# The gate and up stages of a macaron encoder layer: the sums of h taken kind by kind on VectorE, and three direct column blocks in the first stage instead of four

## The chip, the cores and the metric

One core of a Trainium2 chip runs the whole layer in one launch. The metric is the device time of that launch in microseconds, the median of several executions. Engines are named as the profile names them: PE is TensorE, DVE is VectorE, ACT is ScalarE, POOL is GpSimd, and SP is the engine that issues most of the DMAs. L619 and the like are lines of the kernel before.

## The reference, cut to what matters

One layer, batch 1, 1024 tokens, model width 1024, feed-forward width 2816. Three sandwiches follow each other, and the first and the last are feed-forward stages:

```python
def swiglu(h, w_gu, w_down):
    g, u = jnp.split(h @ w_gu, 2, axis=-1)
    return (jax.nn.silu(g) * u) @ w_down

def sandwich(x, fn, g_pre, g_post, shift, scale, gate, res_w):
    h = modulate(rmsnorm(x, g_pre), shift, scale)
    y = rmsnorm(fn(h), g_post)
    return x + res_w * gate[:, None, :] * y
...
x = sandwich(x, ffn1, ...)   # res_w 0.5
x = sandwich(x, mix, ...)    # attention and a recurrent branch
x = sandwich(x, ffn2, ...)   # res_w 0.5
```

The change lies in `h @ w_gu` of both feed-forward stages: `h` is 1024 x 1024, `w_gu` is 1024 x 5632. All is float32.

## The kernel before, in words

Every float32 operand is cut into a high part (an fp32r copy, ScalarE) and a low part (the value less its copy, mostly VectorE), and a product is three matmuls: high by high, low by high, high by low. `hh[k]` and `hl[k]` are the two parts of the k-th 128 rows of `h` transposed, 128 x 1024 (`h1` the first 512 tokens, `h2` the second). The columns of `w_gu` are taken in 22 column blocks `fb` of 128, gate and up together, of which `load` fetches 512 KB for each.

The first blocks are *direct*: `part(fb, sh, k)` (L582) does the six matmuls of one k on one half `sh` of the tokens, so a block has 2 x 8 x 6 = 96 matmuls of 128x128 by 128x512. `finish` (L599) applies Silu on ScalarE, the product with the up half on VectorE, and stores the result. `DIRECT` (L44) says how many: four in the first stage, three in the last. In the first stage blocks 0 to 2 belong to `startup` (L1679), since `h` is only being made; block 3 is done by `up_phase` (L794). In the last stage blocks 0 and 1 are done by `head` (L775), which runs beside the stage ahead of it.

All other blocks are done in Strassen's manner (`block`, L733; the Winograd form). Split in two over rows and tokens, seven products do the work of eight: `product(fb, i, ...)` (L725) has 4 x 3 = 12 matmuls, a block 7 x 12 = 84. The products stand in the order 1, 2, 6, 5, 7, 3, 4 (`ORDER`, L504). They need
- combinations of the weights, made by `mix(fb, i)` (L700): GpSimd adds and subtracts (four 128x512 instructions a block), ScalarE copies the high part, VectorE subtracts for the low part (seven times, L720). `mix(fb + 1, i)` is called in block `fb` after its product i;
- combinations of `h`, made once a stage by `sums()` (L616). With w, x the two token halves of the upper row block `kk` and y, z those of the lower one, kind 5 is x - w, kind 6 is z - (x - w), kind 4 is y - kind 6, and a fourth, z - x, goes by `differences(kk)` (L679) into `hh[kk]`, `hl[kk]`, second half, in place of x. Each of the first three is cut into a tile `hs` (`high` on ScalarE, `low` on VectorE). Product 5 needs kind 5, product 6 kind 6, product 4 kind 4, product 7 the differences.

Three PSUM banks carry a block. Products 1, 6, 7 and 4 go into one of them, `psX`, one after the other, and between them it is read out: ScalarE copies it to `u` after product 1 (L745) and to `v` after product 6 (L752), and VectorE adds it to `pp` after product 7 (L759, recorded as L739, the line of the helper). Product 6, 7 and 4 wait for these three. Product 3 goes into `psZ` after product 5 has been copied out to `pp` by ScalarE (L756).

In the first stage `h` in 32 bits is not kept. `sums()` has GpSimd add `hh` and `hl` back together (`whole`, L619: eight adds of 128x1024, at L623), and VectorE then does all four combinations of one kk before the next. The steps are spread by `sum_step()` over block 1's and 2's second halves (in `startup`, at the end) and block 3's first half; `first_needs` (L812) does what is left, the first seven mixes and the differences in block 3's second half. In the last stage the second half of `h` is kept in 32 bits from the time when it is made (`whole_h`, filled by `evac_h`, L353), and VectorE adds the first half together itself (L639).

The order of each engine's instructions is that in which this code issues them (`manual_schedule`); an engine takes its instructions strictly in that order. Another user of GpSimd in the stage is `all_sums` (L894), which makes combinations of the down-projection's weights and of finished blocks for the stage that follows; `block` calls `next(jobs)` after each product, and each call is at most one GpSimd instruction of 128x512 (L928).

The lines that matter in the profile: L349 cuts `h`, L143/L144 cut the weights of a direct block (ScalarE, and GpSimd for block 3 in the first stage), L486 to L488 are the direct matmuls, L729 to L731 those of the products, L521 is `finish` on VectorE.

Of the kernel before, what the change touches and what calls it, by code (L numbers as in the profile page):

```python
# [10 lines left out]
F32 = mybir.dt.float32  # L11
# [15 lines left out]
KB = D // P  # L27
# [16 lines left out]
DIRECT = {0: 4, 2: 3}  # L44
# [6 lines left out]
def kernel(  # L51
# [301 lines left out]
    def evac_h(sub, sh, k, pt, hh, hl, on_act, with_lo=True, eng=None):  # L353
# [152 lines left out]
    def ffn(sub, w_gu, w_down, hh, hl, xin, xout):  # L506
# [109 lines left out]
        def sums():  # L616
            recon = {}

            def whole(kk):  # L619
                if kk < 4:  # L620
                    recon[kk] = top, bot = t4("top"), t4("bot")
                    for dst, k in ((top, kk), (bot, kk + 4)):
                        nc.gpsimd.tensor_tensor(dst, hh[k].bitcast(F32), hl[k].bitcast(F32), op=ALU.add)  # L623

# [8 lines left out]
            if sub == 2:  # L633
                for kk in range(4):
                    top, bot = whole_h.pop(kk), whole_h.pop(kk + 4)
                    w_, x_, y_, z_ = top[:, h1], top[:, h2], bot[:, h1], bot[:, h2]
                    s1, s2 = tv("hsum"), tv("hsum")
                    for dst, k in ((w_, kk), (y_, kk + 4)):
                        nc.vector.tensor_tensor(dst, hh[k][:, h1].bitcast(F32), hl[k][:, h1].bitcast(F32), op=ALU.add)  # L639
# [5 lines left out]
                    nc.vector.tensor_tensor(z_, z_, x_, op=ALU.subtract)  # L645
                    dif[kk] = z_
                    nc.vector.tensor_tensor(y_, y_, s2, op=ALU.subtract)
                    high(4, kk, y_)
                    yield
                    low(5, kk, s1)  # L650
                    low(6, kk, s2)
                    low(4, kk, y_)
                    yield
                return

            whole(0)
            yield
            for kk in range(4):
                top, bot = recon.pop(kk)
                w_, x_, y_, z_ = top[:, h1], top[:, h2], bot[:, h1], bot[:, h2]  # L660
                s1, s2 = tv("hsum"), tv("hsum")
                nc.vector.tensor_tensor(s1, x_, w_, op=ALU.subtract)
                high(5, kk, s1)
                whole(kk + 1)
                nc.vector.tensor_tensor(s2, z_, s1, op=ALU.subtract)
                high(6, kk, s2)
                yield
                low(5, kk, s1)
                nc.vector.tensor_tensor(y_, y_, s2, op=ALU.subtract)
                high(4, kk, y_)  # L670
                yield
                low(6, kk, s2)
                nc.vector.tensor_tensor(z_, z_, x_, op=ALU.subtract)
                yield
                low(4, kk, y_)
                dif[kk] = z_
                yield

        def differences(kk):  # L679
            nc.scalar.copy(hh[kk][:, h2], dif[kk])  # L680
            nc.vector.tensor_tensor(hl[kk][:, h2], dif[kk], hh[kk][:, h2].bitcast(F32), op=ALU.subtract)
# [93 lines left out]
        def head():  # L775
# [11 lines left out]
            cut(2, 0)  # L787
            cut(2, 1)
            for k in range(KB):
                part(1, 1, k)  # L790
                sum_step()
            finish(1, 1, tu)
# [1134 lines left out]
```

## Time and profile before

| | |
|---|---|
| three runs | 2188.63, 2191.61, 2191.58 us; median 2191.58 |
| the profiled execution | 2188.63 us, of which 2186.8 from its first to its last instruction |
| PE busy | 2144.6 us, 98% |
| DVE busy | 1306.5 us, 60% |
| ACT busy | 1014.0 us, 46% |
| POOL busy | 699.9 us, 32% |
| mean granted TensorE clock | 0.997 |
| first stage, first direct matmul to first Strassen product | 22.28 to 129.21 us |
| one Strassen block without waits | 84 matmuls, 19.1 us |

How to read it: in a timeline, a row has the start and the length in us, the engine, the line, what is written and read, and in brackets how long the engine stood idle before it and what ended that. A matmul's own length (0.39 us) overlaps the next one's; the pace is the distance between starts. In the list of waits a row has who waited for what, the total in us, how often, and the longest.

### The profile page before, as it was taken

How to read it: one execution, taken by the hardware profiler on the slowest of the kernel's cores; microseconds unless marked ns; L12 is line 12 of the kernel's file. 1: busy time of each engine (PE TensorE's matmuls, PEld its weight loads, DVE VectorE, ACT ScalarE, POOL GpSimd, SP SyncE). 2: the span in 40 equal slices, each digit the busy share in tenths (PEclk: the TensorE clock that was granted, in tenths of full speed). 3: DMA queues.
4: the chain of work that ended last, by engine and by line, in shares of the span. 5: the costliest groups of instructions: out<-in, count | busy, mean ns of one | idle time of the engine just before them, and what ended most of it. 6: DMA issues, size and time to landing. Idle time of an engine off the chain costs nothing. (4 is left out here: it accounts for less than half of the span.)

```text
span 2186.8 us, 26725 instructions
## 1 busy us (share of the span) xinstructions
PE 2144.6 (98%) x9973; PEld 1780.1 (81%) x9973; DVE 1306.5 (60%) x1676; ACT 1014.0 (46%) x1570; POOL 699.9 (32%) x514
## 2 busy tenths in 40 slices
PE   7999999999999999999999999999999999999998
PEld 5878788888878888888898988888888888888877
DVE  6676676557367677655236666555686564544466
ACT  4343333334447788611147776436443333334443
POOL 1558895422104111000121120002168884522102
PEclk9999999999999999999999999999999999999999
DMA  9347674459575111276411011464357663347365
GB/s 327 88 164 256 225 260 154 154 192 335 185 249 195 51 51 43 60 241 218 138 49 61 26 56 55 135 207 164 111 192 260 236 219 118 109 151 271 132 232 183
DMA packets 259322, 358.36 MB, mean 164 GB/s; under 512 B 16592, under 2 KB 166264, under 8 KB 259192
## 3 DMA queue, kind: packets, MB, share of 16 engines
q1 hardware_dynamic: 246272, 310.43, 43.0%
q10 hardware_dynamic: 12920, 46.23, 5.4%
q8 instruction: 78, 1.28, 0.2%
q14 instruction: 52, 0.43, 0.1%
HBM read 265.37 MB, written 94.37 MB: 165 GB/s over the span
## 5 line engine op out<-in xcount | busy, mean ns | idle before, releaser
L143 ACT CAST dh<-rawd 128x1024 fp32r<-128x1024 f32 x154 | 161.4, 1054 | 203.3 <-PE pv L990 60.4
L720 DVE TENSOR_TENSOR wm<-raw,wm 128x512 fp32r<-128x512 f32 x152 | 161.0, 1064 | 153.6 <-ACT wm L719 148.3
L144 DVE TENSOR_TENSOR dh<-rawd,dh 128x1024 fp32r<-128x1024 f32 x130 | 163.1, 1259 | 148.1 <-ACT dh L143 139.2
L486 PE MATMUL pj<-hh,wh 128*128 128x512 f32 x574 | 226.4, 395 | 0.0
L487 PE MATMUL pj<-hl,wh 128*128 128x512 f32 x574 | 224.8, 392 | 0.7 <-DVE hl L349 0.6
L488 PE MATMUL pj<-hh,wl 128*128 128x512 f32 x574 | 224.9, 392 | 0.3 <-DVE wl L144 0.3
L990 PE MATMUL px<-dh,dh 128*128 128x512 f32 x608 | 187.5, 390 | 0.5 <-DVE dh L144 0.5
L338 POOL TENSOR_SCALAR rstd<-rstd 128x1 f32<-128x1 f32 x47 | 29.9, 637 | 429.0 <-ACT junk L337 427.6
L990 PE MATMUL pv<-dh,dh 128*128 128x512 f32 x528 | 163.1, 390 | 2.5 <-DVE dh L144 2.5
L143 ACT CAST wh<-raw 128x1024 fp32r<-128x1024 f32 (+1 forms) x88 | 87.1, 993 | 150.5 <-DMA raw<-in_w_in_dram 40.5
L144 POOL TENSOR_TENSOR wl<-raw,wh 128x1024 fp32r<-128x1024 f32 x20 | 48.4, 2424 | 294.4 <-ACT wh L143 249.9
L928 POOL TENSOR_TENSOR act<-act,act 128x512 f32<-128x512 f32 x54 | 86.0, 1592 | 163.2 <-DMA act<-act 118.6
L990 PE MATMUL px<-dh 128*128 128x512 f32 x352 | 137.3, 390 | 0.0
L990 PEld LDWEIGHTS px<-dh,dh 128*128 128x128 f32 x608 | 114.0, 188 | 24.8 <-DVE dh L144 1.2
L487 PEld LDWEIGHTS pj<-hl,wh 128*128 128x128 f32 x574 | 108.4, 189 | 23.8 <-DVE hl L349 1.9
L488 PEld LDWEIGHTS pj<-hh,wl 128*128 128x128 f32 x574 | 108.3, 189 | 23.6 <-DVE wl L144 1.2
L486 PEld LDWEIGHTS pj<-hh,wh 128*128 128x128 f32 x574 | 108.4, 189 | 21.6
L144 DVE TENSOR_TENSOR wl<-raw,wh 128x1024 fp32r<-128x1024 f32 (+1 forms) x68 | 76.4, 1127 | 75.4 <-ACT wh L143 75.3
L990 PEld LDWEIGHTS pv<-dh,dh 128*128 128x128 f32 x528 | 98.8, 188 | 24.4 <-DVE dh L144 4.0
L729 PE MATMUL psX<-hh,wm 128*128 128x512 f32 x296 | 115.5, 390 | 2.7 <-ACT mixes L752 2.7
L729 PE MATMUL psX<-hs,wm 128*128 128x512 f32 x296 | 115.7, 391 | 1.2 <-ACT mixes L745 1.0
L730 PE MATMUL psX<-hs,wm 128*128 128x512 f32 x296 | 115.2, 389 | 0.0
(333 smaller groups left out, 5686.8 us busy)
## 6 DMA issues: line engine op xcount, KB each, us to landing
rawa<-in_w_ada_dram SPq DMA_DIRECT2D x64, 512.0 KB, 5.0
raw<-in_ffn_w_gu_dram SPq DMA_DIRECT2D x47, 512.0 KB, 4.6
rawd<-acts SPq DMA_DIRECT2D x88, 256.0 KB, 4.0
rawd<-downs SPq DMA_DIRECT2D x88, 256.0 KB, 3.6
raw<-in_w_in_dram SPq DMA_DIRECT2D x44, 512.0 KB, 3.8
act<-act SPq DMA_DIRECT2D x37, 512.0 KB, 5.0
acts<-act ACTq DMA_DIRECT2D x36, 512.0 KB, 4.1
sr<-in_ffn_w_gu_dram SPq DMA_DIRECT2D x35, 512.0 KB, 5.9
```

The source lines that it names most:

```text
L143: nc.scalar.copy(hi, raw)
L144: (eng or nc.vector).tensor_tensor(lo, raw, hi.bitcast(F32), op=ALU.subtract)
L338: nc.gpsimd.tensor_scalar(r, r, eps, None, op0=ALU.add)
L486: nc.tensor.matmul(dst, wh[:, kk, :], xhk[:, sl], start=first, stop=False)
L487: nc.tensor.matmul(dst, wh[:, kk, :], xlk[:, sl], start=False, stop=False)
L488: nc.tensor.matmul(dst, wl[:, kk, :], xhk[:, sl], start=False, stop=last)
L720: nc.vector.tensor_tensor(t[:, 1], src, t[:, 0].bitcast(F32), op=ALU.subtract)
L729: nc.tensor.matmul(dst, t[:, 0, kk, :], xh, start=first and kk == 0, stop=False, skip_group_check=True)
L730: nc.tensor.matmul(dst, t[:, 0, kk, :], xl, start=False, stop=False, skip_group_check=True)
L928: nc.gpsimd.tensor_tensor(o, p, q, op=op)
L990: nc.tensor.matmul(dst, a_[:, 0, tk], w_[:, 1, :], start=first and n == 0, stop=last and n == 2, skip_group_check=True,)
```

## The change

- `DIRECT` of the first stage is 3. Block 3 becomes a Strassen block, and `startup` and `head` end in two shared functions, `sum_columns` and `last_columns`.
- In the first stage too, `evac_h` writes the 32-bit second half of `h` into tiles that are kept (`whole_h`). GpSimd's eight adds are gone, and with them block 3's two weight cuts on GpSimd.
- `sums()` is one for both stages and goes kind by kind: kind 5 for all four kk, then kind 6 with the differences, then kind 4. Each of the three has three VectorE instructions a kk, and each `low` stands one kk behind its `high`. The results overwrite the kept tiles, where before there were two scratch tiles.
- In the first stage, the first eight steps (kinds 5 and 6) stand in block 1's second half. Block 2's second half has the seven mixes of block 3 and the four differences between its parts. Kind 4 is left for block 3 itself: `after(i)` calls `sum_step` after each product of the first Strassen block.
- In the last stage, kinds 5 and 6 stand in block 1's second half, kind 4 in block 2's first half with the first four mixes behind it, and the differences in block 2's second half.

Inserted and removed lines move the line numbers: what was L720 in the kernel before is L706 in the changed one, L739 is L725, L719 is L705, L745 is L731, L752 is L738, L756 is L742, L707 is L693, L928 is L914.

```diff
-DIRECT = {0: 4, 2: 3}
+DIRECT = {0: 3, 2: 3}
...
-        if sub == 2 and sh == 1:
+        if sub != 1 and sh == 1:
             whole_h[k] = t4("whole")
             h32 = whole_h[k][:, sl]
...
-            whole(0)
-            yield
             for kk in range(4):
-                top, bot = recon.pop(kk)
-                w_, x_, y_, z_ = top[:, h1], top[:, h2], bot[:, h1], bot[:, h2]
-                s1, s2 = tv("hsum"), tv("hsum")
-                nc.vector.tensor_tensor(s1, x_, w_, op=ALU.subtract)
-                high(5, kk, s1)
-                whole(kk + 1)
-                nc.vector.tensor_tensor(s2, z_, s1, op=ALU.subtract)
-                high(6, kk, s2)
+                w_, x_ = tops[kk][:, h1], tops[kk][:, h2]
+                first_half(w_, kk)
+                vec(w_, x_, w_)
+                high(5, kk, w_)
+                if kk:
+                    low(5, kk - 1, tops[kk - 1][:, h1])
                 yield
...
+            low(5, 3, tops[3][:, h1])
+            for kk in range(4):
+                s1, x_, z_ = tops[kk][:, h1], tops[kk][:, h2], bots[kk][:, h2]
+                vec(x_, z_, x_)
+                dif[kk] = x_
+                vec(z_, z_, s1)
+                high(6, kk, z_)
+                if kk:
+                    low(6, kk - 1, bots[kk - 1][:, h2])
+                yield
+            low(6, 3, bots[3][:, h2])
+            tops.clear()
+            for kk in range(4):
+                y_, s2 = bots[kk][:, h1], bots[kk][:, h2]
+                first_half(y_, kk + 4)
+                vec(y_, y_, s2)
                 high(4, kk, y_)
+                if kk:
+                    low(4, kk - 1, bots[kk - 1][:, h1])
                 yield
...
+        def sum_columns(fb, last, alloc=None):
             for k in range(KB):
-                part(1, 1, k)
+                part(fb, 1, k)
                 sum_step()
...
+        def last_columns(fb):
+            for k in range(KB):
+                part(fb, 1, k)
+                if (direct, ORDER[min(k, 6)]) not in mixed and (k < 4 or sub == 0):
+                    mix(direct, ORDER[min(k, 6)])
+                if k < 4:
+                    differences(k)
+            finish(fb, 1)
...
             for fb in range(direct, NF):
 
                 def after(i):
+                    if fb == direct:
+                        sum_step(2 if i == 5 else 1)
                     mix(fb + 1, i)
                     next(jobs, None)
...
         f1.finish(0, 1)
-        for fb in (1, 2):
-            for k in range(KB):
-                f1.part(fb, 1, k)
-                f1.sum_step()
-            f1.finish(fb, 1)
+        f1.sum_columns(1, False)
+        f1.last_columns(2)
```

Three places show what stands where now. The first is VectorE around the start of the first Strassen block. Before, this is block 4: `hl` are the differences, `wm` the low parts of the mixes, `a` a finished direct block, and `mixes` from `psY` is the sum that follows product 2.

```order
L720 TENSOR_TENSOR wm_1031<-wsum_999,wm_1031 128x512
L681 TENSOR_TENSOR hl_109<-bot_723,hh_101 128x512
L681 TENSOR_TENSOR hl_110<-bot_738,hh_102 128x512
L681 TENSOR_TENSOR hl_111<-bot_781,hh_103 128x512
L681 TENSOR_TENSOR hl_112<-bot_830,hh_104 128x512
L521 TENSOR_TENSOR a_195_1066<-a_195_1066,pj_995 128x512
L720 TENSOR_TENSOR wm_1070<-raw_934,wm_1070 128x512
L720 TENSOR_TENSOR wm_1073<-raw_932,wm_1073 128x512
L720 TENSOR_TENSOR wm_1076<-raw_934,wm_1076 128x512
L720 TENSOR_TENSOR wm_1104<-raw_1079,wm_1104 128x512
L739 TENSOR_TENSOR mixes_1084<-psY_1087,mixes_1084 128x512
```

In the changed kernel the same place is block 3, from the finished block 2 (`a`) on; `whole` and `hs` are sums and low parts of kind 4.

```order
L521 TENSOR_TENSOR a_150_891<-a_150_891,pj_811 128x512
L626 TENSOR_TENSOR whole_650<-hh_105,hl_113 128x512
L626 TENSOR_TENSOR whole_650<-whole_650 128x512
L706 TENSOR_TENSOR wm_952<-raw_922,wm_952 128x512
L725 TENSOR_TENSOR mixes_927<-psY_930,mixes_927 128x512
L626 TENSOR_TENSOR whole_665<-hh_106,hl_114 128x512
L626 TENSOR_TENSOR whole_665<-whole_665 128x512
L623 TENSOR_TENSOR hs_947<-whole_650,hs_947 128x512
L706 TENSOR_TENSOR wm_978<-raw_922,wm_978 128x512
```

The sums of kind 4 now stand between the mixes and the reads of the block's own products. The second place is ScalarE in that block, from the copy of product 1 out of `psX` to the copy of product 5 out of `psZ`. Before:

```order
L745 COPY mixes_1084<-psX_1086 128x512
L719 CAST wm_1104<-raw_1079 128x512
L749 ACTIVATE act_1083<-mixes_1084 128x512
L719 CAST wm_1125<-raw_1079 128x512
L752 COPY mixes_1084<-psX_1086 128x512
L719 CAST wm_1142<-raw_1079 128x512
L756 COPY pp_1085<-psZ_1151 128x512
```

In the changed kernel:

```order
L731 COPY mixes_927<-psX_929 128x512
L619 CAST hs_947<-whole_650 128x512
L705 CAST wm_952<-raw_922 128x512
L735 ACTIVATE act_926<-mixes_927 128x512
L619 CAST hs_975<-whole_665 128x512
L705 CAST wm_978<-raw_922 128x512
L738 COPY mixes_927<-psX_929 128x512
L619 CAST hs_996<-whole_680 128x512
L705 CAST wm_1000<-raw_922 128x512
L742 COPY pp_928<-psZ_1009 128x512
```

Each copy that frees a bank for PE has a cast of `hs` ahead of it now, which needs VectorE's sum of the same kk. The third place is GpSimd around the first mixes of the stage (L707, in the changed kernel L693). Before, they follow the eight adds of 128x1024, of which the last two are shown:

```order
L623 TENSOR_TENSOR top_829<-hh_104,hl_112 128x1024
L623 TENSOR_TENSOR bot_830<-hh_108,hl_116 128x1024
L707 TENSOR_TENSOR wsum_999<-raw_934 128x512
L707 TENSOR_TENSOR raw_934<-raw_932,raw_934 128x512
L707 TENSOR_TENSOR raw_932<-wsum_999,raw_932 128x512
L707 TENSOR_TENSOR raw_932<-raw_932 128x512
L707 TENSOR_TENSOR wsum_1101<-sr_1081 128x512
```

In the changed kernel they are the first instructions after the norms of x, and the piece goes on to the first job (L914, which was L928):

```order
L693 TENSOR_TENSOR wsum_815<-raw_556 128x512
L693 TENSOR_TENSOR raw_556<-raw_533,raw_556 128x512
L693 TENSOR_TENSOR raw_533<-wsum_815,raw_533 128x512
L693 TENSOR_TENSOR raw_533<-raw_533 128x512
L693 TENSOR_TENSOR wsum_949<-sr_924 128x512
L693 TENSOR_TENSOR sr_924<-raw_922,sr_924 128x512
L693 TENSOR_TENSOR raw_922<-wsum_949,raw_922 128x512
L693 TENSOR_TENSOR raw_922<-raw_922 128x512
L914 TENSOR_TENSOR top_955<-top_955 128x512
```

The adds of 128x1024 are gone; all mixes of the first Strassen block and those of the second stand ahead of the jobs, as they did before.

More of the change, by code (lines that the diff above doesn't have):

```diff
@@ L616, in sums @@
         def sums():
[L617 to L623, printed above, removed]
             def high(i, kk, s32):
@@ L656, in sums, with vec @@
-            whole(0)
-            yield
-            for kk in range(4):
-                top, bot = recon.pop(kk)
[L660 to L663, printed above, removed]
-                whole(kk + 1)
-                nc.vector.tensor_tensor(s2, z_, s1, op=ALU.subtract)
-                high(6, kk, s2)
-                yield
-                low(5, kk, s1)
-                nc.vector.tensor_tensor(y_, y_, s2, op=ALU.subtract)
+            def vec(out, p, q, op=ALU.subtract):
+                nc.vector.tensor_tensor(out, p, q, op=op)
@@ L786, in head @@
             finish(0, 1, tu)
-            cut(2, 0)
-            cut(2, 1)
+            if direct > 2:
+                cut(2, 0)
+                cut(2, 1)
+            sum_columns(1, direct == 2, tu)
+        def sum_columns(fb, last, alloc=None):
             for k in range(KB):
-                part(1, 1, k)
+                part(fb, 1, k)
                 sum_step()
-            finish(1, 1, tu)
+                if last and k >= 6:
+                    mix(direct, ORDER[k - 6])
+            if last:
+                for kk in range(4):
+                    differences(kk)
+            finish(fb, 1, alloc)
+        def last_columns(fb):
[6 more added lines that the diff above has]
+            finish(fb, 1)
         def up_phase(started):
@@ L805, in up_phase @@
                     part(fb, 0, k)
-                    sum_step()
-                    if sub == 2 and k > 2 and mixed_first < 4:
-                        mix(direct, ORDER[mixed_first])
-                        mixed_first += 1
+                    if k < 4:
+                        sum_step()
+                    else:
+                        mix(direct, ORDER[k - 4])
                 finish(fb, 0)
-            def first_needs():
-                sum_step(100)
-                for i in ORDER[:4]:
-                    if (direct, i) not in mixed:
-                        mix(direct, i)
-                        yield
-                for kk in range(4):
-                    differences(kk)
-                    yield
-                for i in ORDER[4:]:
-                    mix(direct, i)
-                    yield
-            needs = first_needs()
-            for fb in range(started, direct):
-                for k in range(KB):
-                    part(fb, 1, k)
-                    if fb == direct - 1 and k < (4 if sub == 2 else len(FIRST_NEEDS)):
-                        for _ in range(FIRST_NEEDS[k]):
-                            next(needs)
-                finish(fb, 1)
-            for _ in needs:
-                pass
+            for fb in range(started, direct):
+                last_columns(fb)
+            for i in ORDER:
+                if (direct, i) not in mixed:
+                    mix(direct, i)
             load(direct + 1, 0)
```

36 lines of the change are left out of this document (10 added, 26 removed).

## The prediction

> **What bounds the kernel now.** The profile's page comes first, the span and the engines' shares:
>
> ```profile
> span 2186.8 us, 26725 instructions
> PE 2144.6 (98%) x9973; PEld 1780.1 (81%) x9973; DVE 1306.5 (60%) x1676; ACT 1014.0 (46%) x1570; POOL 699.9 (32%) x514
> ```
>
> PE is busy for 98% of the span, so a change is worth the matmuls that it takes away, less the idle time that it brings. What idle time there is in the stage at hand, the list of waits from 110 to 500 us says (who waited for whom, us in total, times, longest), and under it stands the one wait of the last stage, from the same list for 1570 to 1960 us:
>
> ```profile
> PE psX L729 <- ACT mixes L752: 2.0, 2, 1.1
> PE psZ L729 <- ACT pp L756: 1.8, 1, 1.8
> PE psX L729 <- ACT mixes L745: 1.0, 1, 1.0
> ```
>
> ```profile
> PE psX L729 <- ACT mixes L752: 0.7, 1, 0.7
> ```
>
> PE's timeline says where: block 3's first matmul, the first of block 4 (the first Strassen block), that of its product 2, and the two waits inside it.
>
> ```profile
> 107.45 0.39 PE L486 MATMUL pj<-hh,wh 128*128 128x512 f32 x1
> 129.21 0.39 PE L729 MATMUL psX<-hh,wm 128*128 128x512 f32 x1
> 131.93 0.39 PE L729 MATMUL psY<-hh,wm 128*128 128x512 f32 x1
> 135.83 0.50 PE L729 MATMUL psX<-hs,wm 128*128 128x512 f32 x1 [1.01 <-ACT mixes L745]
> 142.42 0.50 PE L729 MATMUL psX<-hh,wm 128*128 128x512 f32 x1 [0.86 <-ACT mixes L752]
> ```
>
> A product of 12 matmuls takes 131.93 - 129.21 = 2.72 us, so a matmul 0.227. The first Strassen block loses 1.01 + 0.86 = 1.9 us. Why it does, and later blocks don't, the busy times by stretch show, that block first and then the next one:
>
> ```profile
> 129.20:150.20 21.00, 19.13 (x83) 15.20 (x82) 17.09 (x19) 11.19 (x21) 13.81 (x10) 1.00 0.54 180
> 150.20:169.30 19.10, 19.10 (x86) 15.80 (x85) 12.92 (x13) 6.96 (x12) 18.02 (x13) 1.00 0.76 281
> ```
>
> The columns are PE, PEld, DVE, ACT, POOL, each with its count. In an ordinary block VectorE is busy 12.9 of 19.1 us with 13 instructions, in the first 17.1 with 19. VectorE and the two engines that hang on it, ScalarE and GpSimd, are the second bound here.
>
> **Matmuls.** Block 3 becomes a Strassen block: 96 matmuls go, 84 come, 12 x 0.227 = 2.7 us less. On PE's program this is all that changes.
>
> **VectorE's price.** Its timeline, first without GpSimd beside it (a pair of which the second reads what the first wrote, then four in a row), then with it:
>
> ```profile
> 118.71 0.68 DVE L662 TENSOR_TENSOR hsum<-top 128x512 f32<-128x512 f32 x1
> 119.50 0.69 DVE L665 TENSOR_TENSOR hsum<-bot,hsum 128x512 f32<-128x512 f32 x1
> ...
> 132.44 4.66 DVE L681 TENSOR_TENSOR hl<-bot,hh 128x512 fp32r<-128x512 f32 x4
> 137.03 0.67 DVE L521 TENSOR_TENSOR a<-a,pj 128x512 f32<-128x512 f32 x1
> 137.62 2.48 DVE L720 TENSOR_TENSOR wm<-raw,wm 128x512 fp32r<-128x512 f32 x4
> 140.03 0.68 DVE L739 TENSOR_TENSOR mixes<-psY,mixes 128x512 f32<-128x512 f32 x1
> ```
>
> GpSimd just before, alone, and in the same time:
>
> ```profile
> 128.70 1.29 POOL L707 TENSOR_TENSOR raw<-wsum,raw 128x512 f32<-128x512 f32 x1
> ...
> 132.60 1.68 POOL L707 TENSOR_TENSOR wsum<-sr 128x512 f32<-128x512 f32 x1 [1.23 <-DVE wm L720]
> 134.36 1.59 POOL L707 TENSOR_TENSOR sr<-raw,sr 128x512 f32<-128x512 f32 x1
> ```
>
> Alone, four take 140.03 - 137.62 = 2.41 us, 0.60 each; the dependent one starts 0.79 after its writer, 0.19 more. Beside the two of GpSimd, four take 137.03 - 132.44 = 4.59: 2.18 more, 1.09 us of delay for each GpSimd instruction. Where GpSimd stood at 128x1024 it was worse: VectorE started one instruction in 2.8 us, as often as GpSimd did.
>
> ```profile
> 99.31 2.88 DVE L669 TENSOR_TENSOR bot<-bot,hsum 128x512 f32<-128x512 f32 x1
> 102.12 2.88 DVE L631 TENSOR_TENSOR hs<-hsum,hs 128x512 fp32r<-128x512 f32 x1
> ```
>
> ```profile
> 98.80 2.85 POOL L623 TENSOR_TENSOR bot<-hh,hl 128x1024 f32<-128x1024 f32 x1
> ```
>
> That is what the change takes away: eight adds and two weight cuts on GpSimd, for eight adds on VectorE. But PE did not wait for it, since block 3 with its 21.8 us (107.45 to 129.21) lay between the sums and their first use. The change removes this block, so the first use moves to 107.45, and the cover goes with it.
>
> **How late VectorE is.** Its queue in the changed kernel starts behind block 0's store (L521), before:
>
> ```profile
> 86.56 0.69 DVE L521 TENSOR_TENSOR a<-a,pj 128x512 f32<-128x512 f32 x1 [2.71 <-ACT a L520]
> ```
>
> It waited for a Silu on ScalarE, ahead of which stood a cast of block 3's weights, which goes. Block 0's last matmul ends 96 matmuls ahead of 107.45, at 85.7, so I take 86.5 for the end of the store, not 87.2. From there to the sum that stands just ahead of ScalarE's copy `v` in block 3, VectorE has 43 instructions: 24 for kinds 5 and 6, a store, 7 low parts of mixes and 4 differences, a store, two sums of kind 4, a low part of block 4's first mix, the addition after product 2, two more sums. 43 x 0.60 = 25.9 us, 10 of them dependent, 1.9. GpSimd has seven instructions in that time (all four mixes of block 3, three of block 4), whose data are there long before; they wait for VectorE's own low parts, so they fall among its instructions: 7 x 1.09 = 7.6. Once VectorE waits for two casts of ScalarE (a part of kind 4, then the mix) after a sum. What ScalarE needs:
>
> ```profile
> 130.02 0.62 ACT L719 CAST wm<-raw 128x512 fp32r<-128x512 f32 x1 [5.91 <-POOL raw L707]
> 130.55 0.61 ACT L719 CAST wm<-wsum 128x512 fp32r<-128x512 f32 x1
> ...
> 140.75 0.63 ACT L749 ACTIVATE act<-mixes 128x512 f32<-128x512 f32 x1 [4.45 <-DVE mixes L739]
> 141.29 0.60 ACT L719 CAST wm<-raw 128x512 fp32r<-128x512 f32 x1
> 141.79 0.58 ACT L752 COPY mixes<-psX 128x512 f32<-128x512 f32 x1
> ```
>
> 0.53 us a start, so about 1.3 with the handing over. The sum ends at 86.5 + 25.9 + 1.9 + 7.6 + 1.3 = 123.2; a cast of `hs`, a cast of a mix and the copy `v` follow, 1.7: 124.9. PE wants product 7 at 107.45 + 4 x 2.72 = 118.3. So it waits 6.6 us, where it waited 0.86.
>
> Product 7 ends at 127.6. Until then the same two engines have four VectorE instructions (one dependent, one behind a cast, one GpSimd instruction among them: 4.2 us, to 127.4) and then three of ScalarE, the last being the copy of product 5, to 129.1: product 3 waits 1.5 and ends at 131.8. Product 4 waits for VectorE's addition to `pp`, with eight instructions from 127.4: 4.8 + 0.2 + 1.0 for two casts. Now GpSimd's jobs start too; their loads stand in SP's queue behind block 2's store. None of them costs nothing more (133.4, a wait of 1.6), all seven that could be ready cost 7.6 (141.0, 9.2). I take four, since GpSimd is busy 18.0 of 19.1 us in the ordinary block above: 137.8, a wait of 6.0. Together 6.6 + 1.5 + 6.0 = 14.1 us.
>
> **The clock.** A wait of that length costs more. After a long wait PE starts its matmuls more slowly (block 0 to 2's first halves):
>
> ```profile
> 56.44 1.02 PE L267 MATMUL pc<-ones_r,rawa 128*128 128x1 f32 x8 [3.63 <-DVE rawa L260]
> ...
> 57.74 0.77 PE L486 MATMUL pj<-hh,wh 128*128 128x512 f32 x1
> ...
> 60.44 0.92 PE L1711 MATMUL pt<-ident,x 128*128 128x128 f32 x4
> ```
>
> Six matmuls took 60.44 - 57.74 = 2.70 us, 0.45 each, where six need 1.36: 1.3 lost. Two waits over 3.63 us make 2.7. The Trainium skill, "TensorE: Matmul & The Clock Gate", Part 1, says that the clock halves after an idle window of about 3.4 us, free-running, and returns after as long a busy one. By that each costs 1.7 us, an estimate, and the sum would be 0.7 more; by it also a wait between one and two windows may escape.
>
> **Edits that cost nothing.** Keeping `h` in 32 bits writes the same halves by the same instructions to other tiles. Block 4's up weights go into one of these tiles' pool; their load waits for the last transposes of x and stands on SP behind block 0's store, and is wanted by GpSimd after block 3's mixes, past 107: with the 4.6 us that such a load needs it is covered by some 15.
>
> ```profile
> raw<-in_ffn_w_gu_dram SPq DMA_DIRECT2D x47, 512.0 KB, 4.6
> ```
>
> The extra 7 calls of `next(jobs)` lie under PE. In the last stage the 36 instructions of `sums()` stay 36 in the same two stretches, and PE waited 0.7 there: 0, give or take 0.7.
>
> **The sum.** -2.7 for the matmuls, -1.9 for the old waits, +14.1 and +2.7: +12.2 us. The profiled execution (2186.8 between first and last instruction, 1.8 around it) would take 2188.63 + 12.2 = 2200.8. It was the fastest of the three runs; against the median, 2191.58, I predict 2203.8.
>
> **Rivals.**
>
> *GpSimd costs half.* If VectorE, always ready, gets in ahead of GpSimd more often than in the row at 132.44 and a GpSimd instruction delays it by 0.55, `v` comes at 121.1 and the wait is 2.8; the others are 1.2 and 3.0, none long enough for the clock: 7.0 - 4.6 = +2.4 us, 2194.0. For it: in the ordinary block 13 instructions of VectorE take 12.9 us, 0.3 more each than the 0.69 alone. Against it: there VectorE isn't behind. The Trainium skill, "SBUF — State Buffer", section "SBUF: two separate sides", speaks against it: whichever of the two starts first has the shared ports "for the whole instruction". By that a GpSimd instruction costs up to its own length, 1.29 us, and the row at 132.44 is nearer to that than to 0.55.
>
> *VectorE is in time, and the kernel gets faster.* If GpSimd's seven fall where VectorE waits anyway, `v` comes at 86.5 + 25.9 + 1.9 + 1.3 + 1.7 = 117.3, before PE wants it, and the block runs with 0 to 1.2 us of waiting: -2.7 - 1.9 + 0 to 1.2 = -4.6 to -3.4, 2187.0 to 2188.2. It is decided at 118.3: the 7.6 us for GpSimd must shrink to 1.0. For it: GpSimd's work in the stretch is 7 instructions, no longer eight adds of 128x1024 and two cuts. Against it: five of the seven are released by VectorE itself, while its queue is full.
>
> *Block 4 is late too.* If the jobs, the loads that wait for kind 4 (block 5's up weights) and ScalarE's DMA issues keep the queue full for a second block, +18 to +24 us. Against it: from product 4 on VectorE has only an ordinary block's work, and the block after the first of the kernel before lost nothing.
>
> **Chances.** The forecast 0.60 (with GpSimd's price from 0.8 to 1.3 and 0 to 7 jobs, +4.4 to +18.5); half price 0.20 (0 to +5); in time 0.15; block 4 too 0.05. About 0.2%, 4.4 us, is what a measurement can tell here. Slower by more: 0.60 + 0.05 + 0.03 of the half price, 0.68. Within: 0.17 of the half price and 0.07 of the in-time case, 0.24. Faster: 0.08. The range leaves out the in-time case and the late block 4: 2191.5 to 2210.0.
>
> **What would show it.** Right: the sums at 0.60 to 0.79 us a start from 86.5, except beside GpSimd; in the first Strassen block, from 107.45 on, PE waits for ScalarE's copy `v` and for VectorE's addition to `pp`, some 6 us each, with matmuls at 0.45 us behind them, and VectorE never idle from 86 to 135; the next block without waits. Wrong: `v` copied before 118.3, or VectorE's instructions at 0.60 beside GpSimd's; waits in the last stage; a later start of the Strassen blocks than 107.45.

## The result, and the profile after

The changed kernel takes 2208.54 us (median of 4 runs, 2208.14 to 2210.18), the kernel before beside it 2191.6 (2188.63 to 2192.23): a ratio of 1.0087, interval 1.0074 to 1.0100. That is slower by 16.9 us by the medians and by some 19 us by the ratio, which is not that of the two medians, where +12.2 had been forecast. One run of ten of each of two kernels below (four and six tiles kept) took over 5000 us and is left out of their medians. The page of the changed kernel starts with:

```profile
span 2206.3 us, 26722 instructions
...
PE 2148.9 (97%) x9961; PEld 1782.9 (81%) x9961; DVE 1312.4 (59%) x1694; ACT 1017.1 (46%) x1578; POOL 676.6 (31%) x508
```

PE has its 12 matmuls less, and is busy for longer nevertheless: 2148.9 us for 2144.6. VectorE's total grew by 6 us only, GpSimd's fell by 23. So it is not how much the engines do, but when. The list of PE's waits from 105 to 500 us (who waited for whom, us in total, times, longest):

```profile
PE psX L715 <- ACT mixes L738: 9.7, 3, 5.9
PE psX L715 <- DVE pp L725: 6.9, 1, 6.9
PE psZ L715 <- ACT pp L742: 2.4, 2, 2.2
```

The two long ones stand in the first Strassen block, block 3. PE's timeline shows the first matmul of product 7, the last matmul of product 7 and the first of product 4:

```profile
123.90 0.80 PE L715 MATMUL psX<-hh,wm 128*128 128x512 f32 x1 [5.88 <-ACT mixes L738]
...
128.72 0.39 PE L717 MATMUL psX<-hh,wm 128*128 128x512 f32 x1
...
138.80 0.79 PE L715 MATMUL psX<-hs,wm 128*128 128x512 f32 x1 [6.95 <-DVE pp L725]
```

VectorE's timeline shows what they wait for: block 0's store, the first sum of kind 5, block 1's store behind the 24 sums of kinds 5 and 6, three low parts, two sums of kind 4, and the addition that product 4 waits for:

```profile
85.48 0.69 DVE L521 TENSOR_TENSOR a<-a,pj 128x512 f32<-128x512 f32 x1 [1.85 <-PE pj L488]
86.09 0.68 DVE L626 TENSOR_TENSOR whole<-hh,hl 128x512 f32<-128x512 f32 x1
...
103.94 0.68 DVE L521 TENSOR_TENSOR a<-a,pj 128x512 f32<-128x512 f32 x1
...
111.56 4.07 DVE L706 TENSOR_TENSOR wm<-raw,wm 128x512 fp32r<-128x512 f32 x3
...
129.68 1.77 DVE L626 TENSOR_TENSOR whole<-hh,hl 128x512 f32<-128x512 f32 x1
131.49 1.65 DVE L626 TENSOR_TENSOR whole<-whole 128x512 f32<-128x512 f32 x1
...
138.06 0.68 DVE L725 TENSOR_TENSOR pp<-psX,pp 128x512 f32<-128x512 f32 x1
```

Beside the three low parts stand two of GpSimd's mixes, beside the sums of kind 4 its jobs, of which one is shown:

```profile
111.11 1.67 POOL L693 TENSOR_TENSOR wsum<-sr 128x512 f32<-128x512 f32 x1 [1.83 <-DVE wm L706]
112.86 1.62 POOL L693 TENSOR_TENSOR sr<-raw,sr 128x512 f32<-128x512 f32 x1
...
129.29 1.62 POOL L914 TENSOR_TENSOR bot<-bot,top 128x512 f32<-128x512 f32 x1
```

ScalarE's copy `v` comes behind a cast that waited for VectorE's queue, and behind the cast of a mix:

```profile
122.22 0.62 ACT L619 CAST hs<-whole 128x512 fp32r<-128x512 f32 x1 [1.46 <-DVE whole L626]
...
123.27 0.58 ACT L738 COPY mixes<-psX 128x512 f32<-128x512 f32 x1
```

The rest shows in the busy times by stretch (length, then PE, PEld, DVE, ACT, POOL, each with its count, then the granted clock, the DMA share and GB/s). Each stretch runs from one block's product 2 to the next one's: block 3, the ordinary block 7, then blocks 8, 9, 10 and 11.

```profile
109.69:145.99 36.30, 23.47 (x86) 18.44 (x84) 31.37 (x32) 10.46 (x20) 20.89 (x13) 0.81 0.40 131
204.07:223.11 19.04, 19.04 (x85) 15.77 (x84) 11.49 (x17) 6.96 (x12) 16.66 (x12) 1.00 0.67 231
223.11:245.86 22.75, 20.97 (x85) 16.86 (x84) 12.93 (x11) 6.64 (x12) 19.40 (x14) 0.92 0.54 192
245.86:267.25 21.39, 19.34 (x86) 15.69 (x84) 18.27 (x38) 6.64 (x12) 13.26 (x10) 1.00 0.69 216
267.25:290.79 23.54, 21.29 (x85) 16.75 (x84) 12.31 (x12) 6.84 (x12) 17.68 (x13) 0.93 0.75 253
290.79:309.83 19.04, 19.04 (x85) 15.77 (x84) 14.47 (x14) 6.85 (x12) 17.95 (x12) 1.00 0.78 273
```

The same view of the kernel before, for its first Strassen block (4) and for block 10, the only later one that lost much:

```profile
131.93:153.44 21.51, 19.64 (x85) 15.61 (x84) 19.08 (x21) 9.91 (x19) 14.96 (x10) 1.00 0.57 186
249.73:272.70 22.97, 19.93 (x85) 15.54 (x84) 17.52 (x31) 6.64 (x12) 16.24 (x12) 1.00 0.70 237
```

An undisturbed block takes 19.04 us. Block 3 takes 36.30, 17.3 too much: PE is idle for 36.30 - 23.47 = 12.8 us, and its matmuls are 4.4 us slower at a clock of 0.81. Against before this is -2.7 (12 matmuls) - 2.5 (the old first Strassen block's 21.51) + 17.3 = +12.1 us, which is the forecast. Blocks 8 to 10 add something that the forecast didn't have: together 10.6 us too much (3.7, 2.35, 4.5), with 0.96 in block 6 11.5. Before, blocks 6 to 14 lost 5.6 in all, 3.9 of it in block 10. So +5.9 more, and +18.0 in sum. Block 3 starts 0.5 us earlier than before, which says little: in the kernels below with three direct blocks it starts between 106.9 and 109.4 us. At the start of the down products the two profiled executions are 17.5 us apart (498.42 against 480.95); the medians are 16.9 apart.

What blocks 8 and 10 waited for, on ScalarE (its Silu in block 8) and on GpSimd (its first mix in block 10, with product 3's wait at the end of that chain):

```profile
231.54 0.63 ACT L735 ACTIVATE act<-mixes 128x512 f32<-128x512 f32 x1 [7.12 <-DMA downs<-bot]
```

```profile
272.64 1.28 POOL L693 TENSOR_TENSOR wsum<-sr 128x512 f32<-128x512 f32 x1 [6.61 <-DMA sr<-in_ffn_w_gu_dram]
```

```profile
280.88 0.50 PE L715 MATMUL psZ<-hh,wm 128*128 128x512 f32 x1 [2.17 <-ACT pp L742]
```

The first is a store of the jobs that still occupies the tile which `act` is to take, the second a load of up weights that landed late. In block 9 VectorE works off the 24 small instructions of the recurrence's constants (an expectation below counts 22; the stretch has 38 instructions instead of 11 to 17), which the kernel before had in block 10. The jobs run seven calls ahead of the blocks now, the constants one block ahead. Which of the two is to blame, this trace alone does not say.

### The profile page after: what moved, and what is told of

It reads as the page before. It is cut to its first block, busy times and chain, and to the rows that moved or that the text cites. A ratio compares the mean times of both kernels' runs of the same rounds, so it can differ in the third digit from the quotient of the medians.

```text
span 2206.3 us, 26722 instructions
## 1 busy us (share of the span) xinstructions
PE 2148.9 (97%) x9961; PEld 1782.9 (81%) x9961; DVE 1312.4 (59%) x1694; ACT 1017.1 (46%) x1578; POOL 676.6 (31%) x508
## 5 line engine op out<-in xcount | busy, mean ns | idle before, releaser
L706 DVE TENSOR_TENSOR wm<-raw,wm 128x512 fp32r<-128x512 f32 x156 | 162.3, 1043 | 160.6 <-ACT wm L705 153.8
L486 PE MATMUL pj<-hh,wh 128*128 128x512 f32 x542 | 214.0, 395 | 0.0
L487 PE MATMUL pj<-hl,wh 128*128 128x512 f32 x542 | 212.1, 392 | 0.6 <-DVE hl L349 0.6
L488 PE MATMUL pj<-hh,wl 128*128 128x512 f32 x542 | 212.1, 391 | 0.3 <-DVE wl L144 0.2
L914 POOL TENSOR_TENSOR act<-act,act 128x512 f32<-128x512 f32 x54 | 84.9, 1573 | 169.2 <-DMA act<-act 97.9
L144 POOL TENSOR_TENSOR wl<-raw,wh 128x1024 fp32r<-128x1024 f32 x18 | 43.1, 2399 | 288.8 <-ACT wh L143 243.8
L715 PE MATMUL psX<-hh,wm 128*128 128x512 f32 x304 | 120.2, 395 | 10.7 <-ACT mixes L738 10.7
L715 PE MATMUL psX<-hs,wm 128*128 128x512 f32 x304 | 119.8, 394 | 7.2 <-DVE pp L725 6.9
L488 PEld LDWEIGHTS pj<-hh,wl 128*128 128x128 f32 x542 | 102.2, 189 | 22.5 <-DVE wl L144 1.2
L487 PEld LDWEIGHTS pj<-hl,wh 128*128 128x128 f32 x542 | 102.3, 189 | 22.0 <-DVE hl L349 1.5
L717 PE MATMUL psX<-hh,wm 128*128 128x512 f32 x304 | 119.7, 394 | 0.0
L716 PE MATMUL psX<-hl,wm 128*128 128x512 f32 x304 | 119.7, 394 | 0.0
L716 PE MATMUL psX<-hs,wm 128*128 128x512 f32 x304 | 119.1, 392 | 0.0
```

The costliest lines, as they stand in the source:

```text
L144: (eng or nc.vector).tensor_tensor(lo, raw, hi.bitcast(F32), op=ALU.subtract)
L486: nc.tensor.matmul(dst, wh[:, kk, :], xhk[:, sl], start=first, stop=False)
L487: nc.tensor.matmul(dst, wh[:, kk, :], xlk[:, sl], start=False, stop=False)
L488: nc.tensor.matmul(dst, wl[:, kk, :], xhk[:, sl], start=False, stop=last)
L706: nc.vector.tensor_tensor(t[:, 1], src, t[:, 0].bitcast(F32), op=ALU.subtract)
L715: nc.tensor.matmul(dst, t[:, 0, kk, :], xh, start=first and kk == 0, stop=False, skip_group_check=True)
```

## Experiments

The theory: block 3's 21.8 us were cover. Without them VectorE's queue of sums and mixes, with 1.09 us for each GpSimd instruction beside it, is late for products 7 and 4; and the lead of the jobs costs the later blocks some 6 us. The rivals: sums by kind on VectorE are dear in themselves; GpSimd has no part in it; the later blocks are late for another reason. The kernel before took 2190.81 us beside the first four kernels, 2191.16 beside the second four and 2191.14 beside the last three.

**Four direct blocks, sums by kind.** All of the change but the number of blocks:

```
-DIRECT = {0: 3, 2: 3}
+DIRECT = {0: 4, 2: 3}
...
-        f1.last_columns(2)
+        for k in range(KB):
+            f1.part(2, 1, k)
+        f1.finish(2, 1)
```

> The sums by kind on VectorE and the kept h stay, but the first stage has four direct blocks again, so block 3's 21.8 us lie once more between the sums and the first Strassen block. Theory (cover lost): VectorE's 36 sums and the mixes are done before the first Strassen block's products want them; no wait over 2 us in that block, product 7 and product 4 wait under 1.5 us each, and the blocks after it keep the phase that they had before: 2189 to 2194 us, the same as before within 0.2%. Rival (the sums by kind are dear in themselves, wherever the first Strassen block stands): most of the 16.9 us stay, 2200 us or more.

Measured: 2189.75 us, ratio 0.9996 (0.9986 to 1.0005). The first Strassen block doesn't wait at all:

```profile
132.23:151.27 19.04, 19.04 (x85) 15.77 (x84) 10.43 (x14) 6.85 (x12) 14.36 (x10) 1.00 0.60 196
247.24:271.44 24.20, 21.27 (x86) 16.76 (x84) 18.53 (x33) 6.64 (x12) 17.52 (x12) 0.93 0.64 220
```

The rival falls. In the first Strassen block the sums by kind are even the better way (19.04 us for 21.51 before); the block with the constants (second line) takes 1.2 us of these 2.5 back, and the rest lies within the interval of the measurement. Only with the fourth direct block gone is the time lost.

**No jobs in the first Strassen block.**

```
-                    next(jobs, None)
+                    if sub or fb > direct:
+                        next(jobs, None)
```

> The changed kernel, but the first Strassen block of the first stage makes no call of next(jobs), so that GpSimd's seven 128x512 instructions of the jobs do not stand beside VectorE's queue there, and each later block makes the calls that the block of the same number made before. Theory (GpSimd's jobs slow VectorE from 0.6 to 1.7 us an instruction there): product 7 still waits some 5 to 6 us, product 4's wait falls from 6.95 to under 1.5, and with the clock's share the first block gives back 7 to 9 us. Theory on the rest (the +6 us in blocks 8 to 10 come from the jobs being seven calls ahead): these blocks go back to within 1 us of before, another -6: together 2192 to 2196 us. Rival (the later blocks are late because of the earlier start of the blocks itself or of the recurrence's constants): blocks 8 to 10 stay slow, 2199 to 2202. Rival (product 4's wait is VectorE's own queue): it stays over 4 us, 2204 or more.

Measured: 2198.51 us, 1.0030 (1.0020 to 1.0040), 10.0 us less than the changed kernel. Its two waits in block 3:

```profile
126.44 0.79 PE L715 MATMUL psX<-hh,wm 128*128 128x512 f32 x1 [5.96 <-ACT mixes L738]
136.26 0.50 PE L715 MATMUL psX<-hs,wm 128*128 128x512 f32 x1 [1.63 <-DVE pp L725]
```

Product 7's wait stays, product 4's falls from 6.95 to 1.63: the queue behind it was long by the jobs. Block 3 takes 29.68 us, 6.6 less. Blocks 8 and 10 are back at 19.04; but block 9 takes 24.25 and block 14 21.52, so that the blocks from 6 on lose 8.6, not 11.5. The total lies above what I expected of theory and lead together, and under the rivals. It left open whether the lead had cost 3 us or 6.

**No sums of kind 4.**

```
-            for kk in range(4):
+            for kk in range(4 if sub else 0):
                 y_, s2 = bots[kk][:, h1], bots[kk][:, h2]
...
-                t = hs[i, kk]
+                t = hs[6 if i == 4 and not sub else i, kk]
```

> The changed kernel with the sums of kind 4 left out in the first stage (product 4 multiplies the sums of kind 6 instead, so the computation is not the reference's): 12 instructions of VectorE and 4 casts of ScalarE fewer in the first Strassen block, nothing else. Theory (VectorE and ScalarE, in order, are late by what stands in their queues): both waits go, product 7 waits under 1.5 us, product 4 under 1; the first block falls from 36.3 to 19 to 21 us, -15 to -17, while the +6 us of blocks 8 to 10 stay: 2191 to 2195 us. Rival (GpSimd's instructions set the pace, so that the sums fill time which is lost anyway): the waits shrink by less than half, 2200 us or more.

Measured: 2188.43 us, 0.9987 (0.9977 to 0.9996), some 3 us under what was expected. Block 3 takes 20.47 us, with one wait of 1.14, though all the jobs are there:

```profile
111.34:131.81 20.47, 19.33 (x86) 15.69 (x84) 16.65 (x19) 8.09 (x16) 12.57 (x9) 1.00 0.61 195
```

Twelve VectorE instructions and four casts of ScalarE decide 15.8 us, far more than 12 x 0.60: PE's idle time in the block falls from 12.8 us to 1.1, and with the long waits go the slow matmuls, 4.4 us before and 0.3 here. In this kernel the blocks from 6 on lose 8.0.

**The constants one block later.**

```
-                    if i == 3:
+                    if i == 3 and (sub or fb > direct):
                         if next(early, BANK) is BANK and sub == 0:
```

> The changed kernel, but the first Strassen block of the first stage does not start the step of early constants (the loads and sums for the recurrence that are issued once per block), so that these come with the block numbers of before. Theory (the +6 us of blocks 8 to 10 come from the jobs' lead of seven calls): nothing changes beyond 2 us, 2206 to 2210. Rival (they come from the constants' lead of one block): blocks 8 to 10 give back 4 to 6 us, 2202 to 2205.

Measured: 2208.46 us, 1.0079 (1.0064 to 1.0095), against 2208.54 for the changed kernel: no gain. In its profiled execution, its fastest (a span of 2203.6), block 9 was back at 19.04 and block 10 took 23.98; that one trace gave back 3 us in these blocks, the median none.

**No jobs first, and no GpSimd in the first mixes.**

```
+            still = sub == 0 and fb <= direct + 1
             def pool(out, p, q, op):
-                nc.gpsimd.tensor_tensor(out, p, q, op=op)
+                if not still:
+                    nc.gpsimd.tensor_tensor(out, p, q, op=op)
...
-                s1 = first_sum[fb] = tv("wsum", shape=(P, 4, P))
+                s1 = first_sum[fb] = c if still else tv("wsum", shape=(P, 4, P))
```

> The kernel of no_jobs_first, with GpSimd's four instructions left out of the mixes of the first two Strassen blocks of the first stage (the weights of these two blocks are then not the sums that they should be, so the computation is not the reference's): eight GpSimd instructions of 128x512 gone, seven of which lie beside VectorE's queue between block 0's store and the copy that product 7 waits for. Theory (each delays VectorE by 1.09 us): that copy comes up to 7.6 us earlier, product 7's wait of 5.96 us falls under 1, product 4's of 1.63 too, and the kernel gives back 6 to 9 us against no_jobs_first: 2189.5 to 2192.5. Rival (half of that price): the wait falls to some 2 us, 2193 to 2195. Rival (no price; VectorE's own instructions fill the time): it stays over 5 us, 2197 to 2200.

Measured: 2191.04 us, 1.0001 (0.9992 to 1.0010), 7.5 less than without this edit (6.4 by the ratios). Product 7 doesn't wait any more. Product 4, which was to wait less too, waits longer: 2.19 us for 1.63, since PE is there earlier. The copy `v`, in the kernel without jobs first, then in this one:

```profile
125.81 0.58 ACT L738 COPY mixes<-psX 128x512 f32<-128x512 f32 x1
```

```profile
116.34 0.58 ACT L741 COPY mixes<-psX 128x512 f32<-128x512 f32 x1
```

Product 2 of block 3 began at 112.15 and at 109.90, so the copy stands 13.66 and 6.44 us behind it: 7.2 us for seven GpSimd instructions, 1.03 each. In both kernels a cast that waited for VectorE stands two instructions ahead of the copy, so it is the queue that sets its time. The prediction had 1.09, from one row, and the rival 0.55. The Trainium skill, "SBUF — State Buffer", section "SBUF: two separate sides", gives the shared ports to the one that starts first for its whole instruction; by that a GpSimd instruction costs up to its own length, 1.29 us here, and the trace lies near this end.

**First halves of h kept for four tiles.** On top of the kernel without jobs first, the mixes whole again:

```
-        if sub != 1 and sh == 1:
-            whole_h[k] = t4("whole")
+        if sub == 0 and k >= 4 or sub != 1 and sh == 1:
+            if k not in whole_h:
+                whole_h[k] = t4("whole")
...
-                vec(dst, hh[k][:, h1].bitcast(F32), hl[k][:, h1].bitcast(F32), ALU.add)
+                if sub or not (k >= 4):
+                    vec(dst, hh[k][:, h1].bitcast(F32), hl[k][:, h1].bitcast(F32), ALU.add)
```

> The kernel of no_jobs_first, in which the first halves of the last four tiles of h are kept in 32 bits too, so that the four additions of kind 4 that restore them go from VectorE; two of them stand ahead of the copy that product 7 waits for, one between it and product 4. Theory (VectorE's queue sets the end, instruction by instruction): product 7's wait falls by 1.2 to 2.0 us, to 4.0 to 4.8, product 4's by 0.6 to 1.3, the kernel by 2 to 3.5: 2195 to 2196.5 us. Rival (the end is set by ScalarE's casts or by GpSimd): under 1 us, 2197.5 to 2199.

Measured: 2194.61 us, 1.0019 (1.0010 to 1.0029), 3.9 less; product 7 waits 4.50, product 4 1.17. Four additions fewer make 1.5 and 0.5 us less waiting, the first as expected and the second a little less; the total is a little beyond what was expected.

**Six tiles kept, and the sums begun earlier.** On top of the last one, `k >= 2` in place of `k >= 4`, and:

```
             if k + 3 < KB:
                 trans(1, k + 3)
+            if k > 4:
+                f1.sum_step()
         f1.finish(0, 1)
```

> The kernel of no_jobs_first with six tiles of h kept whole (six of the eight additions gone) and the first three steps of the sums moved up into block 0's second half, where VectorE had idle time ahead of block 0's store. Theory: the queue is shorter by 6 x 0.6 and starts 1.85 us earlier, 5.5 us in all, the wait of product 7 falls to under 1.5 us: 2191 to 2193.5 us, at best level with before, as the blocks that are late because of the jobs and the constants stay. Rival (the earlier tiles make the start of the kernel wait, or the sums hold back the low parts that block 0 needs): the first Strassen block starts over 1 us later, 2195 or more.

Measured: 2192.75 us, 1.0007 (0.9997 to 1.0017). Product 6 waits 0.94 and product 7 1.63, block 3 takes 22.21. The block with the constants, however, takes 25.47:

```profile
230.17:255.64 25.47, 21.80 (x85) 17.49 (x84) 18.36 (x38) 6.64 (x12) 15.31 (x12) 0.87 0.74 258
```

So the change is repaired in block 3 to 3.2 us, and what it gains is lost in block 9.

**Jobs ahead with four direct blocks.** The first experiment's kernel, and:

```
                     next(jobs, None)
+                    if sub == 0 and fb == direct + 1:
+                        next(jobs, None)
```

> The kernel of four_by_kind, in which block 5, the second Strassen block, makes two calls of next(jobs) per product instead of one, so that from block 6 on the jobs are seven calls ahead, as in the changed kernel. Theory (the lead of the jobs makes loads and tiles of the later blocks late): blocks 6 to 12 lose 3 to 7 us more than in four_by_kind, 2193 to 2197 us, with waits that end with a load or a store of the jobs. Rival (the later losses have nothing to do with the lead): 2189 to 2191.

Measured: 2204.44 us, 1.0065 (1.0050 to 1.0080), 14.7 more than without this edit, twice what I expected. The losses begin in the doubled block itself (152.84) and peak in the one behind it:

```profile
152.84:175.28 22.44, 19.38 (x86) 15.69 (x85) 11.22 (x12) 6.74 (x12) 15.93 (x12) 1.00 0.88 310
175.28:205.73 30.45, 21.56 (x85) 17.03 (x84) 13.39 (x13) 6.74 (x12) 24.31 (x18) 0.89 0.72 243
```

In the worst block, as in block 10 of the changed kernel, GpSimd's first mix waited for up weights that landed late, and product 3 stands at the end of that chain:

```profile
187.72 1.26 POOL L693 TENSOR_TENSOR wsum<-sr 128x512 f32<-128x512 f32 x1 [5.44 <-DMA sr<-in_ffn_w_gu_dram]
```

```profile
195.51 0.79 PE L715 MATMUL psZ<-hh,wm 128*128 128x512 f32 x1 [7.96 <-ACT pp L742]
```

These two blocks lose 14.8 us, blocks 7 to 10 lose 7.7, against 5.6 without the edit. The experiment shows that the jobs move the time, but does not part two causes, the doubled calls and the lead that stays behind them.

**No jobs in the second Strassen block.** The changed kernel, with the jobs back in their old places from block 5 on, and block 3 as it is:

```
-                    next(jobs, None)
+                    if sub or fb != direct + 1:
+                        next(jobs, None)
```

> The changed kernel, whose second Strassen block (block 4) makes no call of next(jobs); the first one does, so that its waits stay, and from block 5 on the jobs stand where they stood before. Theory (the lead of the jobs makes blocks 8 to 10 late, some 3 us of the 6): the first block stays at 36 us, blocks 8 and 10 go back to 19 to 20 us, block 9 with the constants takes 24: 2204 to 2206.5 us. Rival (the lead is not the cause): 2207.5 to 2209.5.

Measured: 2203.06 us, 1.0061 (1.0048 to 1.0073), 5.5 less than the changed kernel. Its blocks 3, 7, 8, 9 and 10:

```profile
109.61:146.02 36.41, 23.67 (x85) 18.56 (x84) 30.90 (x32) 10.47 (x20) 17.59 (x11) 0.81 0.40 134
203.57:222.61 19.04, 19.04 (x85) 15.77 (x84) 12.86 (x18) 6.95 (x12) 16.97 (x12) 1.00 0.74 255
222.61:241.65 19.04, 19.04 (x85) 15.77 (x84) 11.76 (x11) 6.84 (x12) 18.57 (x13) 1.00 0.50 186
241.65:264.26 22.61, 19.35 (x85) 15.69 (x84) 19.47 (x38) 6.64 (x12) 14.65 (x12) 1.00 0.80 279
264.26:283.40 19.14, 19.14 (x86) 15.69 (x84) 11.21 (x11) 6.85 (x12) 16.93 (x12) 1.00 0.72 250
```

Block 3 is the same, blocks 8 and 10 lose nothing, and the blocks from 6 to 14 lose 5.7 together, as before the change (5.6). So in the changed kernel the lead of seven calls costs 5.5 us, a little more than I expected. It is no fixed price: with the same lead, blocks 7 to 10 of the last experiment lost 2.1 more than without it, and the blocks from 6 on in the kernel without kind 4 2.4 more than before.

**The constants spread.** Their block was the largest loss left in the repaired kernel (block 9) and in the kernel before (block 10). With their instructions spread over five blocks, on top of the repaired kernel (six tiles kept, sums earlier, no jobs first), and on the kernel before, alone:

```
         for q in (11, 9, 7, 5, 3, 1):
+            if q in (11, 7, 3):
+                yield
             v.tensor_tensor(pl, pl, s2, op=ALU.mult)
             v.tensor_scalar(pl, pl, 1.0 / q, None, op0=ALU.add)
+        yield
```

> The kernel of skip_keep_early (three direct blocks, 2192.78 us), with the 22 small VectorE instructions of the recurrence's constants spread over five blocks instead of one. Theory (that burst holds VectorE, then ScalarE, then product 7 in block 9, which took 6.4 us too long there): this block's 25.5 us fall to under 21, and the kernel to 2186 to 2189 us, faster than before by 0.1 to 0.2%. Rival (the block is late because of the jobs' loads and stores, and the burst falls into time that is lost anyway): no gain over 1.5 us, 2191 or more.

> The kernel before (four direct blocks), with the same spreading of the constants and nothing else, so that the three direct blocks are compared at equal constants. Theory: its block 10, 3.9 us too long, gives back 2.5 to 4 us: 2187 to 2189, level with repaired_spread within 2 us, since that one saves 2.7 us of matmuls and 2.5 us of the old waits and still loses some 3 us in its first Strassen block and in others. Rival: no gain, 2190 to 2192.

Measured: 2185.37 us, 0.9978 (0.9969 to 0.9987), and 2188.22 us, 0.9987 (0.9978 to 0.9996). The repaired kernel's blocks 3 and 9:

```profile
111.86:134.06 22.20, 19.62 (x85) 15.61 (x84) 18.58 (x22) 10.34 (x20) 9.75 (x7) 1.00 0.33 95
...
230.72:249.76 19.04, 19.04 (x85) 15.77 (x84) 16.07 (x21) 6.74 (x12) 15.04 (x12) 1.00 0.84 304
```

Block 9 falls from 25.47 to 19.04, and the kernel by 7.4 us. It is the first with three direct blocks and nothing left out that beats the kernel before, by 5.8 us by the medians. Its blocks fit that: -2.7 for the matmuls, -2.5 + 3.2 for the first Strassen block, and the blocks from 6 to 14 lose 1.7 instead of 5.6, -3.9; in sum -5.9. Its profiled execution as a whole doesn't: it is 2.3 us above its median, the one before 2.5 to 3 under its own, and the two spans differ by 0.9 only. About half of the gain has nothing to do with the change, since the kernel before gets 2.9 us by the same spreading. What remains for three direct blocks with their repairs is 2.9 us by the medians and 2 by the ratios; the intervals overlap by half.

## Where the prediction was right, and where it was wrong

**Right: the cover and the place, and by some luck the size.** The terms for the first Strassen block came to +14.1 of waits, +2.7 of clock, -2.7 and -1.9: +12.2. The trace has 12.8 of idle time, 4.4 of slower matmuls, -2.7 and -2.5: +12.1. VectorE's store ended at 86.2 (I took 86.5), `v` was copied by 123.9 (124.9), product 7 waited 5.88 (6.6) and product 4 6.95 (6.0). The runs without kind 4 and with four direct blocks show that it is this queue and this cover.

**Right: GpSimd's price.** 1.03 us for each instruction by the run without the first mixes, 1.09 forecast; "GpSimd costs half" falls.

**Errors that cancelled.** Product 3 was to wait 1.5 and did not, since PE itself came later: its clock was low for longer than I had assumed. 11 matmuls took 128.72 - 123.90 = 4.82 us where they need 2.50, so the first wait cost 2.3 more, and all slow matmuls of the block 4.4, not 2.7. The step "Two waits over 3.63 us make 2.7" was sized by six matmuls that did not show the whole slow stretch. Product 4's wait came out near by luck too. From the sum ahead of `v` to the addition, eight GpSimd instructions slowed VectorE's queue and not five (one and the four jobs that I took), which is some 3 us more; but the queue was there 1.1 us earlier, and VectorE waited 0.6 us for casts where 1.5 had been put in.

**Wrong: a cost put at nothing.** The step that failed is "The extra 7 calls of `next(jobs)` lie under PE". I had weighed only GpSimd's time beside block 3. But the calls are not extra, they are early: every later job, with its loads, its stores and the tiles that they hold, stands seven calls ahead of the blocks, and a Silu then waits for a tile whose store isn't done, and a mix for a load that came late. The blocks from 6 on lost 5.9 us more in the trace, and the kernel gained 5.5 when the lead was taken back in the second Strassen block. With +12.1 the trace has 18.0, where the medians have 16.9. So the forecast of +12.2 fits the first Strassen block alone; the whole change cost 4.7 us more than that by the medians, and near 7 by the ratio.

**The rivals.** "VectorE is in time, and the kernel gets faster" was decided where the prediction put it: `v` was copied by 123.9 and not before 118.3, and only without the first mixes' GpSimd instructions is it there before product 7 wants it. "Block 4 is late too" did not happen: blocks 4 and 5 take 19.04 us each. That blocks 8 and 10 would be late stood in no rival. In the last stage PE waits 1.1 us for these copies where it waited 0.7, within what was forecast.

**The block with the constants.** It loses 2.35 us in the changed kernel, 3.6 without jobs in the second block, 5.2 without jobs in the first and 6.4 with six tiles kept. The traces show from what. The last small instruction, and product 7's wait, in the changed kernel and with six tiles kept:

```profile
251.91 0.16 DVE L1105 TENSOR_SCALAR sp_hx<-colsB 128x8 f32<-128x8 f32 x1
...
256.24 0.50 PE L715 MATMUL psX<-hh,wm 128*128 128x512 f32 x1 [2.06 <-ACT mixes L738]
```

```profile
237.84 0.16 DVE L1108 TENSOR_SCALAR sp_hx<-colsB 128x8 f32<-128x8 f32 x1
...
242.16 0.79 PE L717 MATMUL psX<-hh,wm 128*128 128x512 f32 x1 [3.67 <-ACT mixes L740]
```

Counted from the block's product 2, that last instruction starts at 6.05, 7.25, 7.27 and 7.67 us in the four kernels, and product 7 waits 4.0 us less than that: 2.06, 3.26, 3.27 and 3.67. The rest is slower matmuls: 0.3, 0.3, 1.9 and 2.8 us.

**Still open.** Why the small instructions take longer in one kernel than in another was not traced. The last 2 us between the two profiled executions lie in the down products behind the stage, 201.4 us for 199.1. They need not come from the change: in the thirteen traces this stretch takes 199.1 to 201.6, the longest in the kernel before with its constants spread.

## What to carry to other kernels

A block of work that seems to cost only itself may be the cover of another engine's queue: before it is removed, count what that queue holds from its last free moment to the first use, each GpSimd instruction beside it included. Work that is paced by the block (one call per product) changes its phase against all later loads and tiles when the first block moves; that is a cost of its own, to be taken back by starting it where it started. And when several kernels lose time in the same later block, look at what stands there, and spread it.

## What the hardware showed beyond that

Short waits already brought the low clock, and not at once. In block 8 of the changed kernel PE waited 1.78 us, ran five matmuls at nearly full pace, and only then fell to 0.43 us a matmul, for 3.4 us:

```profile
233.21 0.50 PE L715 MATMUL psX<-hh,wm 128*128 128x512 f32 x1 [1.78 <-ACT mixes L738]
233.55 0.39 PE L716 MATMUL psX<-hl,wm 128*128 128x512 f32 x1
...
234.88 0.63 PE L715 MATMUL psX<-hh,wm 128*128 128x512 f32 x1
235.31 0.63 PE L716 MATMUL psX<-hl,wm 128*128 128x512 f32 x1
...
237.44 0.60 PE L715 MATMUL psZ<-hh,wm 128*128 128x512 f32 x1
```

Without the mixes' GpSimd instructions a wait of 2.19 us brought the low clock too, while waits of 2.06 (block 9) and 3.08 us (without kind 4) passed with less than 0.4 us lost. Two waits of nearly the same length in block 9 part just so: 3.26 us without jobs in the second block passed, 3.27 us without jobs in the first brought the low clock. So it isn't the length alone that decides; that it is the moment at which a wait falls is a guess that fits, and no run tests it. Where waits of 1.8 to 3.3 us brought the low clock, the block's matmuls were 1.9 to 2.3 us slower: of the 10.6 us that blocks 8 to 10 lost, 4.5 were slower matmuls. The Trainium skill, "TensorE: Matmul & The Clock Gate", Part 1, speaks of a free-running window of about 3.4 us that must be idle; the length agrees with the trace, but a wait of half a window was enough here.
